# RWKV-7 stage of a hybrid decoder: 32x32 inverses by transposes on VectorE, smaller projection pieces, and two engines in written order

## The chip, the cores and the metric

The kernel runs on one core of a Trainium2 chip. The metric is the device time of one execution in microseconds. The engines are TensorE (PE; PEld is its weight load), VectorE (DVE), ScalarE (ACT), GpSimd (POOL) and SyncE (SP); ACTq, SPq and POOLq are the DMA issues in those engines' queues.

## The reference

Two decoder layers of width 1024 over 256 positions. Each layer is a SwiGLU block, a mixer and a second SwiGLU block, each followed by a LayerNorm. The mixer of layer 0 is a gated spatial MLP, that of layer 1 is RWKV-7 with 16 heads of 64. The change touches the latter alone:

```python
def step(state, inp):                       # per position t, per head
    r_t, w_t, k_t, v_t, a_t, b_t = inp
    sa = jnp.einsum('bhij,bhj->bhi', state, a_t)
    state = (state * w_t[:, :, None, :] + sa[..., None] * b_t[:, :, None, :]
             + v_t[..., None] * k_t[:, :, None, :])
    y = jnp.einsum('bhij,bhj->bhi', state, r_t)
    return state, y
...
r, k, v = jnp.einsum('nbsd,nde->nbse', x_rkv, w_rkv)
...
y = (y - mean) * lax.rsqrt(var + GN_EPS) * gn_g.reshape(H, N) + gn_b.reshape(H, N)
bonus = jnp.sum(r_h * k_h * r_k, axis=-1, keepdims=True) * v_h
out = ((y + bonus).reshape(bsz, seq, d).astype(x.dtype) * g) @ w_o
```

## The kernel before

The stages run in the order f00, sgu, f01, f10, rwkv, f11 (f = SwiGLU block). The 256 positions are two row blocks m of 128 partitions. Weights come through a stream of 512 KB pieces on the SP queue with four raw slots (L94); most are split into a rounded part wh (ScalarE, L118) and a rest wl (VectorE, L119), and a product takes three matmuls (L221 to L223). The R and V projections of RWKV use the raw fp32 piece directly (L301).

The recurrence is computed in four chunks of 64 positions (ch = 2m + c). Within a chunk the state update is a triangular system for each head; its matrix is inverted in 32x32 blocks. `ab` makes the matrix on TensorE (L988) and masks it on VectorE (L974) into Aab. GpSimd's DMAs write the diagonal blocks to DRAM (dA), and `inv_load` (ScalarE's queue) reads them back as M with one block of 32x32 per partition. Then 31 steps (i0 to i30, L1034 and L1036) run on VectorE for all 128 blocks at once. `inv_out` sends the inverse H, and its transposed copy (L1049), through DRAM (dH, dG) back to the head layout as Hf and G. `od` and `oe` (offdiag, L1079, and offdiag2, L1094) are the products that fill the off-diagonal block of each 64x64 inverse.

For each chunk there are then: `sc` (score matrices, L1013, masked into A), `x` (state times query, L1138), `av` (L1129), `u` (inverse times X, L1155, to VU), `s` (next state, L1165 and L1171), `rs` and `y` (outputs, L1148 and L1178). X<-X,mm (L1140) is the addition on VectorE that `u` of a chunk waits for. Behind them, for each row block, come `on` (group norm in two halves e of the heads: sum L1219, subtract L1221, square on ScalarE L1222, sum L1224, the power -0.5 on GpSimd L259, multiply L1227), `bo` (value times bonus, vb, L931), `og` (L1234 to L1236), `ga` (output gate, L1206), `oc` (transposes) and the output product `O` (eight k for each m). `rdone` ends an R projection: it multiplies R by the decay Ep and computes the bonus (L906 to L909). `dc` (decay_x) makes the shifted decay Ex by DMAs in ScalarE's queue (L821, L822).

What sets the order: a table ORDER of operation names is the order in which the stage's instructions are written. PE and the SP queue keep it. VectorE, ScalarE and GpSimd are ordered by a scheduler that may move an instruction ahead of others that it doesn't depend on. In the names, the digits are m, then c or the column half, then a piece: R011 is piece 1 of half 0 of block 1.

Of the kernel before, what the change touches and what calls it, by code (L numbers as in the profile page):

```python
# [56 lines left out]
class Stream:  # L57
# [80 lines left out]
class Builder:
# [529 lines left out]
    def rwkv(self, S):  # L668
# [230 lines left out]
        def rdone(h):  # L899
            def f(m, ps):  # L900
                if h == 0:
                    st["R"][m] = (st["E"][m][0], self.small(f"bonus{m}", [P, NH]))
                R, bo = st["R"][m]
                rk = self.s4("rk")[:, 0:512]
                s = slice(h * 512, h * 512 + 512)
                V.tensor_tensor(R[:, s], ps, st["E"][m][0][:, s], op=ALU.mult)  # L906
                V.tensor_tensor(rk, ps, st["kp"][m][:, s], op=ALU.mult)
# [115 lines left out]
        def inv_load():  # L1023
            st["M"] = self.s4("M")
            DI.dma_start(st["M"], self.dA.rearrange("b s t -> b (s t)"))

        def inv_step(s):
            def f():
                if s == 0:
# [4 lines left out]
                V.tensor_tensor(tv, H3[:, 0:s + 1, s:s + 1].broadcast_to([P, s + 1, n]),  # L1034
                                M3[:, s:s + 1, s + 1:32].broadcast_to([P, s + 1, n]), op=ALU.mult)
# [51 lines left out]
        def offdiag2(m):  # L1087
            def f():
                Q = st["Q"]
                ps = self.tpb()  # L1090
# [6 lines left out]
                for e in range(2):
                    d0 = e * 64
                    V.tensor_copy(st["Hf"][m].rearrange("p (b t) -> p b t", t=64)[d0:d0 + 32, :, 32:64],
                                  ps[d0:d0 + 32, :].rearrange("p (b t) -> p b t", t=32))  # L1100
# [5 lines left out]
        class Chunk:  # L1106
# [18 lines left out]

            def av(c_):
# [292 lines left out]
```

## Time and profile before

| | before |
|---|---|
| time, median of 3 runs | 1145.75 us (1145.54 to 1149.62) |
| the profiled execution | 1143.73 us, span 1142.0 us |
| TensorE | busy 1103.9 us (97% of the span), mean granted clock 0.988 |
| VectorE | busy 698.7 us (61%) |
| ScalarE | busy 480.5 us (42%) |
| GpSimd | busy 42.2 us (4%) |
| RWKV stage | 724.9 to 946.1 us from the span's start |

Busy time is the time in which at least one instruction of the engine runs. [...] A stretch of TensorE has lost time where it is not busy or where its clock is below 1.00.

### The profile page before, as it was taken

The numbers are of one execution on the slowest core, as the hardware profiler recorded it, in microseconds if no ns is written. First come the engines' busy times: TensorE is split into PE (matmuls) and PEld (weight loads), VectorE is DVE, ScalarE is ACT, GpSimd is POOL, SyncE is SP. The second block draws the span as 40 slices with busy tenths as digits, with TensorE's granted clock in tenths as the row PEclk, the third lists the DMA queues.
The fourth block names the chain that finished last, engine by engine and source line by source line (L and its number), as shares of the span: only waits on it lengthen the run. The fifth ranks groups of instructions, "written<-read, shape, count | busy, mean of one in ns | idle before, by whom it ended". The sixth has DMA issues, their size and how long they took to land.

```text
span 1142.0 us, 15347 instructions
## 1 busy us (share of the span) xinstructions
PE 1103.9 (97%) x5860; PEld 879.1 (77%) x5860; DVE 698.7 (61%) x969; ACT 480.5 (42%) x636; POOL 42.2 (4%) x44
## 2 busy tenths in 40 slices
PE   8999999999999999999999999999989889999997
PEld 5888888778888788888888888775555668788885
DVE  6654556769658555457655453878655787555544
ACT  5544443455335444444444452462123245444430
POOL 0000000100000000000000000112100110000000
PEclk9999999999999999999999999999999989999999
DMA  8776565775645766655677563437876146766530
GB/s 289 236 235 185 185 197 168 232 268 196 208 148 155 240 206 198 186 183 157 197 221 225 183 202 124 166 93 256 271 203 237 43 129 191 239 204 196 184 111 38
DMA packets 153933, 216.51 MB, mean 190 GB/s; under 512 B 21213, under 2 KB 114845, under 8 KB 153858
## 3 DMA queue, kind: packets, MB, share of 16 engines
q1 hardware_dynamic: 152394, 210.80, 57.7%
q0 software_dynamic: 1024, 3.15, 1.0%
q10 hardware_dynamic: 440, 1.57, 0.4%
q8 instruction: 46, 0.75, 0.3%
q14 instruction: 29, 0.24, 0.1%
HBM read 209.46 MB, written 3.42 MB: 186 GB/s over the span
## 4 chain that ended last, share of the span: by engine, by line
PE 81%; DVE 7%; DMA 5%; issue 2%; ACT 2%; POOL 1%; ACTq 0%; SPq 0%; DVEq 0%; POOLq 0%
PE mm L221 15%; PE mm L223 15%; PE mm L222 15%; PE acc L221 8%; PE acc L222 8%; PE acc L223 8%; PE mm L301 3%; DMA raw<-ffn_w_in 2%; DVE wl L119 2%; PE tp L415 2%; POOL rs L259 1%; PE tp L235 1%; ACT wh L118 1%; DMA raw<-rwkv_w_rkv 1%; PE tp L577 1%
## 5 line engine op out<-in xcount | busy, mean ns | idle before, releaser
L119 DVE TENSOR_TENSOR wl<-raw,wh 128x1024 fp32r<-128x1024 f32 (+1 forms) x332 | 396.2, 1209 | 267.1 <-ACT wh L118 259.8
L118 ACT CAST wh<-raw 128x1024 fp32r<-128x1024 f32 (+1 forms) x332 | 340.3, 1041 | 340.8 <-PE acc L223 146.0
L221 PE MATMUL mm<-wh,xh 128*128 128x512 f32 x832 | 327.3, 393 | 5.5 <-ACT wh L118 2.4
L222 PE MATMUL mm<-wl,xh 128*128 128x512 f32 x832 | 324.7, 390 | 0.6 <-DVE wl L119 0.6
L223 PE MATMUL mm<-wh,xl 128*128 128x512 f32 x832 | 325.1, 391 | 0.2 <-DVE xl L228 0.2
L221 PEld LDWEIGHTS mm<-wh,xh 128*128 128x128 f32 x832 | 156.5, 188 | 41.5 <-ACT wh L118 3.9
L223 PEld LDWEIGHTS mm<-wh,xl 128*128 128x128 f32 x832 | 156.6, 188 | 34.6 <-DVE xl L228 1.9
L222 PEld LDWEIGHTS mm<-wl,xh 128*128 128x128 f32 x832 | 156.7, 188 | 33.1 <-DVE wl L119 1.3
L221 PE MATMUL acc<-wh,hT 128*128 128x512 f32 x352 | 141.4, 402 | 0.0
L222 PE MATMUL acc<-wl,hT 128*128 128x512 f32 x352 | 137.4, 390 | 0.0
L223 PE MATMUL acc<-wh,hT 128*128 128x512 f32 x352 | 137.4, 390 | 0.0
L404 ACT ACTIVATE h<-mm 128x256 f32<-128x256 f32 x88 | 33.8, 384 | 106.0 <-PE mm L223 105.9
L223 PEld LDWEIGHTS acc<-wh,hT 128*128 128x128 f32 x352 | 66.1, 188 | 14.8
L222 PEld LDWEIGHTS acc<-wl,hT 128*128 128x128 f32 x352 | 66.2, 188 | 12.6
L221 PEld LDWEIGHTS acc<-wh,hT 128*128 128x128 f32 x352 | 66.1, 188 | 12.7
L405 DVE TENSOR_TENSOR h<-h,mm 128x256 f32<-128x256 f32 x88 | 36.8, 418 | 59.8 <-ACT h L404 59.8
L301 PE MATMUL mm<-raw,mix 128*128 128x512 f32 x128 | 59.4, 609 | 0.9 <-DMA raw<-rwkv_w_rkv 0.9
L259 POOL TENSOR_TENSOR rs<-ve,mhalf 128x1 f32<-128x1 f32 x14 | 14.2, 1011 | 926.2 <-DVE ve L267 926.2
L301 PEld LDWEIGHTS mm<-raw,mix 128*128 128x128 f32 x128 | 23.6, 193 | 26.6 <-issue 23.8
L228 DVE TENSOR_TENSOR hT<-tp,hT 128x512 fp32r<-128x512 f32 x44 | 30.2, 686 | 7.6 <-ACT hT L227 7.6
L227 ACT CAST hT<-tp 128x512 fp32r<-128x512 f32 x44 | 25.9, 588 | 9.0 <-PE tp L415 8.9
L227 ACT CAST xh<-tp 128x512 fp32r<-128x512 f32 x24 | 13.2, 588 | 34.9 <-PE tp L235 34.9
(193 smaller groups left out, 884.2 us busy)
## 6 DMA issues: line engine op xcount, KB each, us to landing
raw<-ffn_w_in SPq DMA_DIRECT2D x352, 256.0 KB, 4.0
raw<-ffn_w_out SPq DMA_DIRECT2D x88, 512.0 KB, 4.2
raw<-rwkv_w_rkv SPq DMA_DIRECT2D x40, 512.0 KB, 3.9
raw<-sgu_w_in SPq DMA_DIRECT2D x32, 512.0 KB, 5.6
raw<-sgu_w_out SPq DMA_DIRECT2D x16, 512.0 KB, 4.3
raw<-rwkv_w_o SPq DMA_DIRECT2D x8, 512.0 KB, 3.4
lng<-ln_g SPq DMA_DIRECT2D x6, 512.0 KB, 6.0
lnb<-ln_b SPq DMA_DIRECT2D x6, 512.0 KB
```

Of the source, the lines that this page charges most:

```text
L118: i = nc.scalar.copy(h[:, s], raw[:, s])
L119: j = nc.vector.tensor_tensor(l[:, s], raw[:, s], h[:, s].bitcast(F32), op=ALU.subtract)
L221: i = mm(out, lhsT=lh, rhs=rh, start=start, stop=False)
L222: mm(out, lhsT=lh, rhs=rl, start=False, stop=False)
L223: mm(out, lhsT=ll, rhs=rh, start=False, stop=stop)
L227: i = self.nc.scalar.copy(h, src)
L228: return i, self.nc.vector.tensor_tensor(l, src, h.bitcast(F32), op=ALU.subtract)
L259: self.nc.gpsimd.tensor_tensor(rs, v, self.mhalf[:, :w], op=ALU.pow)
L301: i = self.nc.tensor.matmul(ps, lhsT=xs[:, c], rhs=h[:, s], start=kk == 0, stop=kk == 7)
L404: nc.scalar.activation(hb[:, o + 256:o + 512], ps[:, 0:256], AF.Silu)
L405: nc.vector.tensor_tensor(hb[:, o:o + 256], hb[:, o + 256:o + 512], ps[:, 256:512], op=ALU.mult)
L415: nc.tensor.transpose(ps[:, o:o + P], st["h"][c][:, hh:hh + P], self.ident)
```

## The change

Five things are done in the RWKV stage.
1. The three round trips through DRAM (dA, dH, dG, 21 DMAs) are replaced by three transposes of 32x32 blocks on VectorE: M<-D before the steps, G<-H and Hd<-H behind them. `ab` masks into D (diagonal) and Aof (off-diagonal) in 128x256 pieces; ScalarE copies 32 rows of Aof into D. `inv_fill` (hf0, hf1) copies Hd into Hf, four copies on VectorE and four on GpSimd. The zeroing of Hf goes to GpSimd, and one half of oe's copy to ScalarE.
2. The R and V projections are emitted in quarter units (one weight piece) instead of half units, at new places among the chunks. In the chunks, `x` now stands ahead of `av`, so that X<-X,mm adds the result of av.
3. ScalarE copies an R projection out of PSUM (rk); the multiplication with Ep (`rm`) and the bonus (`rb`) are operations with places of their own.
4. The DMAs for Ex go into the SP queue instead of ScalarE's.
5. From iload on, each VectorE and ScalarE instruction of this stage is chained behind the one written before it (class Ordered). Weight splits, the splits of transposed blocks (xh, xl) and LayerNorms are not in this chain, and GpSimd's instructions are not.

```diff
+class Ordered:
+    def __getattr__(self, name):
+        fn = getattr(self.eng, name)
+
+        def f(*args, **kw):
+            i = fn(*args, **kw)
+            if self.on:
+                if self.last is not None:
+                    self.b.after(i, self.last)
+                self.last = i
+            return i
+        return f
...
+        V, A = Ordered(self, nc.vector), Ordered(self, nc.scalar)
...
-                masked(t[:, half(c)], ps, self.mask[:, 0:64])
...
-                        DA.dma_start(self.dA[b0:b0 + 16].rearrange("b s t -> s b t"),
-                                    t3[r0:r0 + 32, :, blk * 32:blk * 32 + 32])
+                p3 = ps.rearrange("p (b t) -> p b t", b=8)
+                for out, k in ((Of, 32), (D, 0)):
+                    V.tensor_tensor(out.rearrange("p (b t) -> p b t", b=8), p3[:, :, k:k + 32],
+                                    self.mask[:, k:k + 32].unsqueeze(1).broadcast_to([P, 8, 32]), op=ALU.mult)
+                for e in range(2):
+                    r = slice(e * 64 + 32, e * 64 + 64)
+                    A.copy(D[r, :], Of[r, :])
...
-            DI.dma_start(st["M"], self.dA.rearrange("b s t -> b (s t)"))
+            V.on = A.on = True
+            V.transpose(st["M"].rearrange("p (s t) -> p t s", s=32), st["D"].rearrange("p (b t) -> p t b", b=32))
...
+            (V.transpose(t.rearrange("p (b s) -> p s b", b=32), H.rearrange("p (s t) -> p s t", s=32)))
+            st["G"] = t
+            st["Hd"] = self.s4("Hd")
+            V.transpose(st["Hd"].rearrange("p (b t) -> p t b", b=32), H.rearrange("p (s t) -> p t s", s=32))
...
+                (V.tensor_copy if e else G.tensor_copy)(out, src)
...
-        DX, DW, DA, DI, DO = A, nc.sync, G, A, nc.sync
+        DX, DW = nc.sync, nc.sync
...
-                    for i in range(2):
+                    for i, us in enumerate(((0, 1), (2, 3)) if n == 1 else ((0,), (1,), (2,), (3,))):
...
-u1 rs1 ga01 s1 cR11 sc100 y0 vu11 sc101 y1 av2 sc110 x2 rs2 u2 sc111 un0 on00 on01 og00 y2 bo10 s2 av3 ga10 og01 x3
+mixG11 u1 R113 rb01 hf1 s1 g1_1 mixV10 y0 rm10 rm11 cR10 mixV11 y1 V010 cR11 V011 sc100 g2 p:gn_b V012 sc101 on00 V013 p:gn_g V110 on01 rb10 V111 bo00 rb11 V112 bo01 V113
+vu10 x2 av2 rs2 u2 vu11 s2 sc110 x3 sc111 ga00 av3 rs3 u3 gb ga01 un0 og00 y2 y3 og01 oc00 on10 O00 O10 on11 oc01 O20
```

Three places of the order matter. In the rows of the order, a row is one instruction: its number on its engine, its line, operation, outputs <- inputs and size; "x4" stands for four alike. Line 148 is the helper in class Ordered.

The first is VectorE where the inversion begins. Before, rows 550 to 557: the last mask of Aab, the mixes for later projections, what ends an R projection, and then the first step.

```order
550 L974 TENSOR_TENSOR Aab_6392<-tp,mask 128x512
551 L761 SCALAR_TENSOR_TENSOR mix_6490<-xx_5912,muT,xf_5911 128x128
552 L761 SCALAR_TENSOR_TENSOR mix_6378<-xx_5912,muT,xf_5911 128x128 x4
553 L906 TENSOR_TENSOR Ep_5936<-mm,Ep_5936 128x512
554 L907 TENSOR_TENSOR rk_6479<-mm,kp_5908 128x512
555 L908 TENSOR_TENSOR rk_6479<-rk_6479,r_k_6281 128x512
556 L909 TENSOR_REDUCE bonus_6327<-rk_6479 128x8
557 L1034 TENSOR_TENSOR T_6435<-H_6271,M_6433 128x31
```

After, the same place on VectorE:

```order
542 L148 TENSOR_TENSOR Aof_6271<-tp,mask 128x256
543 L148 TENSOR_TENSOR D_6270<-tp,mask 128x256
544 L148 TENSOR_TENSOR Aof_6271<-tp,mask 128x256
545 L148 TENSOR_TENSOR D_6270<-tp,mask 128x256
546 L148 STREAM_TRANSPOSE M_6411<-D_6270 128x32x32
547 L148 TENSOR_TENSOR T_6413<-H_6260,M_6411 128x31
```

The first step now stands right behind the last mask and the transpose; the mixes and the bonus have moved behind the inversion, and the multiplication of Ep into its middle.

The second place is VectorE ahead of the addition for chunk 2 (u2 waits for it). Before, rows 654 to 661: sums of the group norm of block 0, two masks of a score set, a subtraction, the addition, and the rest of the norm behind it.

```order
654 L1219 TENSOR_REDUCE sa<-acc 128x8 x2
655 L1220 TENSOR_SCALAR sa<-sa 128x8 x2
656 L974 TENSOR_TENSOR A_7218<-tp,mask 128x512
657 L974 TENSOR_TENSOR A_7219<-tp,mask 128x512
658 L1221 TENSOR_TENSOR yc_7301<-acc,sa 128x8x64
659 L1140 TENSOR_TENSOR X<-X,mm 128x512
660 L1221 TENSOR_TENSOR yc_7301<-acc,sa 128x8x64
661 L1224 TENSOR_REDUCE sb<-o_7302 128x8
```

After, 26 instructions stand between the masks of sc101 (rows 644 and 645) and the addition (row 672): the two halves of the norm, rows 646 to 657, the bonus rb10, rows 658 to 660, and these:

```order
661 L119 TENSOR_TENSOR wl_7149<-raw_7146,wh_7148 128x1024
662 L148 TENSOR_TENSOR vb_7174<-vb_6254,bonus_6320 128x512
663 L119 TENSOR_TENSOR wl_7171<-raw_7168,wh_7170 128x1024
664 L148 TENSOR_TENSOR vb_7174<-vb_7174,gn_b_7104 128x512
665 L148 TENSOR_TENSOR rk_6563<-rk_6563,kp_6053 128x512
666 L119 TENSOR_TENSOR wl_7185<-raw_7182,wh_7184 128x1024
667 L148 TENSOR_TENSOR rk_6563<-rk_6563,r_k_6852 128x512
668 L119 TENSOR_TENSOR wl_7202<-raw_7193,wh_7201 128x1024
669 L148 TENSOR_REDUCE bonus_6562<-rk_6563 128x8
670 L148 TENSOR_TENSOR vb_7174<-vb_6254,bonus_6320 128x512
671 L148 TENSOR_TENSOR vb_7174<-vb_7174,gn_b_7104 128x512
672 L148 TENSOR_TENSOR X<-X,mm 128x512
```

The norm is now whole ahead of the addition, and so are four weight splits of the output product and four vb products. Their weight pieces take the slots of the last V pieces.

The third place is TensorE between the last score set of chunk 2 and u2. Before, rows 3291 to 3296: scores, x, rs and u with nothing between.

```order
3291 L1013 MATMUL tp<-ZR_6315,KBT_6225 128x128 x8
3292 L1138 MATMUL mm<-S,ZR_6315 64x64 x8
3293 L1138 MATMUL mm<-S,ZR_6316 64x64 x8
3294 L1148 MATMUL acc<-S,ZR_6315 64x64 x8
3295 L1148 MATMUL acc<-S,ZR_6316 64x64 x8
3296 L1155 MATMUL tp<-X,Hf_6157 64x64 x16
```

After, the same place (L320 is a quarter unit, L1156 is x; av, rs and u of chunk 2 follow):

```order
3265 L1043 MATMUL tp<-ZR_6307,KBT_6219 128x128 x8
3266 L320 MATMUL mm<-raw_6976,mix_7022 128x512 x2
3267 L320 MATMUL mm<-raw_7074,mix_7022 128x512 x2
3268 L320 MATMUL mm<-raw_7084,mix_7022 128x512 x2
3269 L320 MATMUL mm<-raw_7108,mix_7022 128x512 x2
3270 L320 MATMUL mm<-raw_7139,mix_7022 128x512 x2
3271 L1156 MATMUL mm<-S,ZR_6306 64x64 x8
3272 L1156 MATMUL mm<-S,ZR_6307 64x64 x8
```

Five quarter units of V now stand there.

## Rows read from the trace of the kernel before

**Rows 1.** Windows: stretch, length, busy us of PE PEld DVE ACT POOL, PEclk, DMA, GB/s.
```profile
724.90:849.60 124.70, 115.29 (x626) 71.96 (x625) 94.67 (x220) 43.47 (x81) 17.66 (x20) 0.99 0.66 213
849.60:893.90 44.30, 40.90 (x726) 30.35 (x726) 23.18 (x36) 13.25 (x18) 0.00 (x0) 0.88 0.59 191
893.90:909.10 15.20, 11.04 (x212) 8.73 (x212) 13.03 (x23) 2.42 (x5) 3.61 (x2) 1.00 0.11 38
909.10:946.10 37.00, 32.50 (x182) 25.27 (x183) 30.11 (x44) 15.67 (x19) 5.05 (x3) 0.91 0.39 121
```

**Rows 2.** The timeline at 742 to 751: start, duration, engine, line, operation [idle before].
```profile
743.44 1.33 ACTq L821 DMA_DIRECT2D Ex<-Ep  x1
...
746.51 0.62 ACT L227 CAST mh<-mix 128x512 fp32r<-128x512 f32 x1 [2.61 <-DMA Ex<-Ep]
...
747.62 1.12 PE L799 MATMUL acc<-a,ah 65*128 65x512 f32 x2 [1.49 <-ACT ah L790]
```

**Rows 3.** The windows again: three short stretches.
```profile
748.00:754.00 6.00, 6.00 (x17) 4.00 (x16) 4.52 (x13) 4.53 (x7) 1.43 (x1) 0.72 0.03 10
852.00:860.00 8.00, 6.81 (x186) 6.31 (x181) 2.73 (x4) 1.69 (x4) 0.00 (x0) 0.50 0.83 270
932.00:938.00 6.00, 6.00 (x21) 4.75 (x20) 5.54 (x9) 2.23 (x4) 0.00 (x0) 0.59 0.30 87
```

**Rows 4.** The timeline of VectorE and TensorE around the inversion.
```profile
799.60 0.68 DVE L974 TENSOR_TENSOR Aab<-tp,mask 128x512 f32<-128x512 f32 x1
...
809.40 0.69 DVE L906 TENSOR_TENSOR Ep<-mm,Ep 128x512 f32<-128x512 f32 x1 [7.80 <-PE mm L301]
...
812.05 0.18 DVE L1034 TENSOR_TENSOR T<-H,M 128x31 f32<-128x31 f32 x1
...
838.59 0.22 DVE L1036 TENSOR_TENSOR H<-H,T 128x31 f32<-128x31 f32 x1
...
849.57 0.22 PE L1079 MATMUL tp<-G,Aab 32*32 32x32 f32 x2 [1.23 <-DMA G<-dG]
```

**Rows 5.** The chain of waits: start, duration, engine and work.
```profile
810.14 0.66 PE tp L235 x4
...
840.59 6.46 DMA dG<-M
...
847.53 2.51 DMA G<-dG
...
910.25 1.06 PE tp L1206 x2
...
912.36 2.01 PE acc L1178 x32
```

**Rows 6.** The groups by line of the stage, TensorE: busy us, mean ns | idle before.
```profile
L301 PE MATMUL mm<-raw,mix 128*128 128x512 f32 x128 | 59.4, 609 | 0.9 <-DMA raw<-rwkv_w_rkv 0.9
...
L1013 PE MATMUL tp<-ZR,KBT 64*128 64x128 f32 x128 | 10.5, 286 | 3.2 <-DVE VU L1160 1.6 <-ACT KBT L968 0.9 <-ACT ZR L953 0.7
```

**Rows 7.** The groups by line of the stage, VectorE.
```profile
L119 DVE TENSOR_TENSOR wl<-raw,wh 128x1024 fp32r<-128x1024 f32 x20 | 24.0, 1218 | 1.4 <-ACT wh L118 1.4
...
L974 DVE TENSOR_TENSOR A<-tp,mask 128x512 f32<-128x512 f32 x16 | 10.3, 686 | 4.1 <-PE tp L1013 3.9
...
L1049 DVE COPY M<-H 64x1024 f32<-64x1024 f32 x1 | 1.1, 1055 | 0.0
```

**Rows 8.** The timeline at 889 to 912, around the update of chunk 2.
```profile
894.45 0.63 ACT L1222 ACTIVATE o<-yc 128x512 f32<-128x512 f32 x1 [0.51 <-DVE yc L1221]
...
898.45 1.94 POOL L259 TENSOR_TENSOR rs<-sb,mhalf 128x8 f32<-128x8 f32 x1 [0.95 <-DVE sb L1225]
...
900.43 0.69 DVE L1227 TENSOR_TENSOR yc<-yc,rs 128x512 f32<-128x512 f32 x1 [1.53 <-POOL rs L259]
...
901.90 1.15 PE L1165 MATMUL tp<-VU,KB 128*64 128x64 f32 x32 [1.68 <-DVE A L974]
```

**Rows 9.** The timeline of TensorE at 925 to 934.
```profile
931.40 1.94 PE L235 MATMUL tp<-ident,o 128*128 128x128 f32 x8 [3.82 <-DVE o L1236]
```

More of the change, by code (lines that the diff above doesn't have):

```diff
@@ L902, in f, with rmul, rbonus @@
                     st["R"][m] = (st["E"][m][0], self.small(f"bonus{m}", [P, NH]))
[L903 to L907, printed above, removed]
+                    st["rk", m] = self.s4("rk")
+                s = half(h)
+                A.copy(st["rk", m][:, s], ps)
+            return f
+        def rmul(m, h):
+            def f():
+                R, s = st["R"][m][0], half(h)
+                (V.tensor_tensor(R[:, s], st["rk", m][:, s], R[:, s], op=ALU.mult))
+            return f
+        def rbonus(m, h):
+            def f():
+                s = half(h)
+                rk, bo = st["rk", m][:, s], st["R"][m][1]
+                (V.tensor_tensor(rk, rk, st["kp"][m][:, s], op=ALU.mult))
                 V.tensor_tensor(rk, rk, st["r_k"][:, s], op=ALU.mult)
@@ L1124, in vu, with x @@
                 return st["VU"][c_.ch][rows, h * 64:h * 64 + 64]
+            def x(c_):
+                c_.X = self.small("X", [P, 512])
+                if c_.ch:
+                    ps, S0 = self.mmb(), st["S", c_.ch]
+                    for h in range(NH):
+                        mm(ps[par(h), col(h)], lhsT=c_.zr(h, 0), rhs=S0[par(h), col(h)], start=True, stop=True,
+                           tile_position=((h % 2) * 64, (h % 2) * 64))
+                    A.copy(c_.X, ps)
             def av(c_):
@@ L1130, in av @@
                        tile_position=(c_.c * 64, (h % 2) * 64))
-                X = c_.X = self.small("X", [P, 512])
-                A.copy(X, ps)
-            def x(c_):
                 if c_.ch:
-                    ps, S0 = self.mmb(), st["S", c_.ch]
-                    for h in range(NH):
-                        mm(ps[par(h), col(h)], lhsT=c_.zr(h, 0), rhs=S0[par(h), col(h)], start=True, stop=True,
-                           tile_position=((h % 2) * 64, (h % 2) * 64))
                     V.tensor_tensor(c_.X, c_.X, ps, op=ALU.add)
+                else:
+                    A.copy(c_.X, ps)
             def rs(c_):
@@ L1389 @@
 ORDER = """
-p:k_k cm00 cm01 l1_0 lw00 mixK00 flush mixK01 K000 K001 cm10 cm11 la00 lw01 dec00 p:k_a dec01 dc0 mixK10 p:gn_g
-l1_1 mixV00 la01 la10 lw10 mixK11 K010 kp00 K011 lw11 zb00 kp10 K100 K101 kp01 dec10 zb01 cZ00 K110 hz cB00 dw0
-dec11 dc1 K111 zb10 la11 kp11 mixV01 V000 kn10 cB10 mixR00 mixG00 cB01 mixR01 V001 g1 zb11 ih kn11 kn00 cZ01 p:r_k
-ab00 R000 mixG01 cZ10 R001 cZ11 cB11 ab01 cR00 mixR10 V100 ab10 ab11 iload i0 g1_0 mixG10 R100 i1 i2 i3 R101 dw1
-mixV10 p:gn_b kn01 i4 cR01 i5 st0 mixG11 mixV11 V010 cK00 sc000 V011 i6 i7 i8 rs0 i9 kb1 g2 cK10 cK11 i10 i11 V101
-g1_1 cK01 i12 i13 i14 sc001 V110 i15 sc010 i16 kb0 V111 i17 mixR11 i18 i19 i20 i21 i22 i23 i24 i25 st1 vu00 sc011
-i26 i27 ga00 i28 i29 av0 vu01 x0 i30 iout R010 od0 od1 oe0 bo00 oe1 bo01 u0 gb R011 s0 R110 cR10 av1 vu10 x1 R111
-u1 rs1 ga01 s1 cR11 sc100 y0 vu11 sc101 y1 av2 sc110 x2 rs2 u2 sc111 un0 on00 on01 og00 y2 bo10 s2 av3 ga10 og01 x3
-rs3 u3 ga11 bo11 y3 oc00 O00 O10 on10 on11 oc01 O20 un1 og10 O30 og11 xw O40 O50 O60 O70 oc10 ln0 oc11 O01 O11 O21
+p:k_k cm00 cm01 l1_0 lw00 mixK00 flush mixK01 K000 K001 cm10 cm11 la00 lw01 dec00 p:k_a dec01 mixK10
+l1_1 mixV00 la01 la10 lw10 mixK11 dc0 K010 kp00 K011 lw11 zb00 kp10 K100 st0 K101 st1 kp01 dec10 zb01 cZ00 K110 cB00 dw0
+dec11 dc1 K111 zb10 la11 kp11 mixV01 V000 V001 kn10 cB10 mixR00 mixG00 cB01 mixR01 V002 V003 zb11 ih kn11 kn00 cZ01
+ab00 R000 R001 mixG01 cZ10 R002 R003 cZ11 cB11 ab01 mixR10 rm00 mixR11 ab10 ab11 iload i0 i1 cR00 R100 R101 i2 i3 cK00 i4 i5 i6
+cK10 V100 V101 i7 i8 kn01 i9 cK01 V102 V103 i10 i11 R102 R103 dw1 i12 i13 i14 hz R010 R011 i15 i16 rm01 cR01 i17 i18 i19 i20 sc000 R012 R013 i21 i22 i23
+cK11 i24 i25 rs0 kb0 vu00 kb1 R110 R111 i26 i27 i28 i29 i30 iout sc001 g1 od0 hf0 od1 oe0 x0 av0 oe1 u0 g1_0 vu01 sc010 p:r_k s0 sc011 x1 mixG10 rb00 R112 av1 rs1
+mixG11 u1 R113 rb01 hf1 s1 g1_1 mixV10 y0 rm10 rm11 cR10 mixV11 y1 V010 cR11 V011 sc100 g2 p:gn_b V012 sc101 on00 V013 p:gn_g V110 on01 rb10 V111 bo00 rb11 V112 bo01 V113
+vu10 x2 av2 rs2 u2 vu11 s2 sc110 x3 sc111 ga00 av3 rs3 u3 gb ga01 un0 og00 y2 y3 og01 oc00 on10 O00 O10 on11 oc01 O20
+bo10 ga10 O30 un1 bo11 ga11 og10 xw O40 og11 O50 O60 O70 oc10 ln0 oc11 O01 O11 O21
 O31 O41 O51 O61 O71
```

95 lines of the change are left out of this document (38 added, 57 removed).

## Prediction

> **What bounds the kernel now.** [...] The diff touches the RWKV stage alone, so I cut that stage, from its first transpose at 724.9 us to the next stage's first at 946.1, into four stretches by the table of windows [rows 1]. In each, idle is length less PE busy, and clock loss is length times (1 - PEclk), which is rough but adds up:
> - up to the off-diagonal product (od0) at 849.6: 9.4 idle, 1.2 clock;
> - to the update matmul of chunk 2 (u2) at 893.9: 3.4 and 5.3;
> - u2 to u3 at 909.1: 4.2 and 0;
> - u3 to the end of the stage: 4.5 and 3.3.
> Together 31.3 us. PE executes the same matmuls before and after, so the forecast is what becomes of these 31.3.
>
> Then the timeline at the waits. At 747.62 PE waits 1.49 for ah, because ScalarE's queue holds the Ex transfers: the first issue takes 1.33 us there, and the next cast starts 2.61 late, behind DMA Ex<-Ep [rows 2]. The clock then averages 0.72 for 6 us, 1.7 us lost [rows 3]. The inversion (31 steps on VectorE) starts at 812.05 although the last mask that it needs starts at 799.60; VectorE is idle for 7.80 of that, and what ends the idle time is a projection [rows 4]. The last step ends at 838.8, and od0 starts only at 849.57, after a wait of 1.23 on G<-dG [rows 4]; on the chain between them stand two transfers, 6.46 and 2.51 us [rows 5]. Projections hide most of this hole. Last, from 893.9 on there are no projections left to put between the chunks, and each short wait on VectorE shows.
>
> **The change, up to od0.** Gone are the round trips through DRAM and the 12.45 us between mask and first step. In their place: a transpose (M) before the steps and one (G) behind them. The trace of before has no such operation. Lower bound: L1049, a copy with swapped axes of 64x1024, 1.06 us [rows 7]; upper bound: twice that of a whole split (L119, 128x1024, 1.22 [rows 7]), 2.4. I take 1.1, since all three stream 1024 elements per partition. [...]
>
> VectorE from the end of ab11 on PE: two half-width masks and backlog about 2.5, the ScalarE copy into D about 0.5, M 1.1, the steps 22.9 (838.8 - 812.05 [rows 4] less the 6 score masks of that time at about 0.64), Em and Ep products 1.3, two score masks 1.3, G 1.1: 30.7. PE meanwhile has 14 quarter units. One unit is 4 matmul records; 32 units take 59.4 us in all [rows 6], 1.86 each, so 26.0. With six groups of four transposes (0.66 each [rows 5]) and two score sets (16 records each; 8 sets take 10.5 [rows 6], so 1.3 each) it comes to 32.6 at most, some 30 where they overlap. The two sides are level; I let PE lose 1 there. The Ex transfers move to the SP queue, behind and before weight loads; the stream runs up to four loads ahead, which hides some 5 us of issue (8 issues of 0.4 to 1.3); with that cover gone a load would be late by up to 3. The wait at 747 goes, with its clock loss. What other short waits remain, with 777 and the like, I put at 1.8. So **10.6 becomes 2.8: -7.8** (bounds -4.5, if the transposes cost 2.4 and SP delays a load by 1; -10.6, if nothing waits).
>
> Hidden by other engines' slack: 8 copies of D and 4 of rk on ScalarE, which is busy 43.47 of 124.7 us there [rows 1]; the Hf zeroing moved to GpSimd, which works 17.66 of 124.7. Without that slack they would add some 5 us to the mask path. The Hf copies by VectorE and GpSimd, the latter with no row of their kind (a VectorE 512-wide pass 0.69 [rows 7] below, GpSimd's 1.94 for a power [rows 8] above), have od0, od1, oe0 and av0 as cover, some 8 us.
>
> **od0 to u2.** Here the ten quarter units that are kept back (R112, R113 and V010 to V113) fill what PE waited for. I take idle 3.4 to 1, and leave the clock loss: the 32x32 matmuls of od and oe are still there, and the window 852 to 860 stood at 0.50 [rows 3]. **-2.4** (bounds 0 and -7, if the clock holds too).
>
> **u2.** This is where the written order bites. Between the masks of score set sc101 and the addition X<-X,mm that u2 waits for, VectorE before has only bits of the group norm on00/on01, chosen by the scheduler between urgent things. After, it must first go through all of on00, on01, rb10, the rest of rb11, four weight splits and four vb products. Each norm half is a chain through three engines: sum 0.65, scale 0.15, subtract 0.65, ScalarE's square 0.63 [rows 8], sum 0.65, scale 0.15, GpSimd's power 1.94 [rows 8], multiply 0.69, with hand-overs 5.8; in before VectorE waited 1.53 at its end [rows 8], and that was with other work between. Sum: masks 1.3, two halves 11.6, rb10 1.9, four splits 4.9 (1.22 each [rows 7]), four vb 2.5, three bonus operations 1.9, the addition 0.65: 24.7 us. PE has from the end of sc101: five quarter units 9.3, then x2, av2 and rs2, 32 small matmuls each as the set at 901.90 with its 1.15 [rows 8]: 12.7. So **PE stands for about 12 at u2**, where before lost 4.2 in the whole stretch [rows 1]. Behind u2 nothing of that is left on VectorE, and u2 to u3 should run without a wait. +7.8. A long wait before small matmuls cost clock at 931, after 3.82 idle [rows 9]: 0.59 over 6 us [rows 3], 2.5 lost; after 1.62 to 1.68 us (901.90 [rows 8]) nothing. I take half, +1.3. **u2: +9.1** (bounds +5 and +14).
>
> **The tail.** From u3 VectorE owes: VU 0.65, og0 3.8, four splits 4.9, two xl 1.3, on10 and on11 one behind the other 11.6, four vb 2.5, og1 3.8, one more split 1.2: 29.8. PE before took 18.5 from u3 to its wait (931.40 - 3.82 - 909.10) [rows 9]; after it has y2 (2.01) and two gates (2 x 1.06 each) [rows 5] more there: 24.7. oc10 waits about 5.1 against 3.82, since before on10 and on11 were interleaved, and oc00 or oc01, now closer behind their norms, some 0.7. Clock loss as before. **+2.0** (0 to +4).
>
> **Sum.** -7.8 - 2.4 + 9.1 + 2.0 = +0.9. The profiled execution took 1143.73 us (span 1142.0), 0.2% under the median of 1145.75; I add to the median: 1146.65, **1147**.
>
> **Rivals.**
> *The early gain wins (faster).* If the clock also holds through od and oe (5.3 back), because chunk 0 and 1 now have quarter units among them, and the norm halves go faster (power 1.66 rather than 1.94, hand-overs hidden): -5 to -8 more, 1139 to 1142, with all waits before od0 gone 1137. For it: the clock was at 1.00 from 893.9 to 909.1 despite 4.2 idle [rows 1]. It decides when the wait at u2 is under about 6 us: then the net is -5.7, or 0.5%, which is what a measurement here can tell from no change.
> *u2 decides (slower).* One mechanism: the stand of 12 us drops the clock, and u2, s2, x3, av3, rs3, u3 and the y products (some 17 us) then run at half of it; I let 7 of the 17 be lost, not all the 8.5: +7 rather than +1.3, so 1152.5; if VectorE comes late to sc101's masks by 3, 1156. Against it: the same clock row of 893.9 to 909.1. It decides when the wait is over about 16.
> *Transposes or shared ports (slower or same).* At 2.4 us each, two lie on the path to od0: +2.6, 1149.3. VectorE copying with GpSimd at once may also make them take turns: 4 copies of 0.69 and 4 of up to 1.94 one by one instead of side by side, +2.7 before u0, partly covered: 1149. [...]
> *The written order does nothing.* If the scheduler's order was the same, the u2 term falls away. The order of the rows shows that it is not.
>
> **How the numbers follow.** Even, within 0.5% (1140 to 1151.5): 0.42, with the transposes' rival inside. Faster: 0.33, as the early gain is direct and the clock at od unknown. Slower: 0.25. Range 1137 to 1156: from the faster rival with all waits gone to the slower with late masks. The likeliest case's own range is 1142 to 1151.
>
> **What would show it.** Right: first step near 795, od0 near 823, M, G, Hd at about 1.1 each; PE's longest wait at u2, 10 to 13 us, ended by X<-X,mm; oc10 waiting 6; no wait at 747 and at G. Wrong: od0 later than 828 (steps, or D, late); a wait at u2 under 6; a clock of 0.50 over more than 8 us behind it; waits on weight loads, which SP's added issues would cause.

## The result, and the profile after

The changed kernel takes 1154.87 us (median of 6 runs, 1151.88 to 1157.76), the kernel before 1145.12 (median of 6, 1143.35 to 1149.62). The ratio is 1.0081, 95% interval 1.0055 to 1.0108: slower by 0.8%. The forecast was 1147 with a range of 1137 to 1156. The range holds, the likeliest case does not: the time lies in the slower case, which had a chance of 0.25, between the 1152.5 and 1156 of its rival "u2 decides". All times and ratios here are of runs in the usual state; one execution of e4 (1392.61 us, mean clock 0.75) was in a slow one and is left out.

The profiled execution has a span of 1150.9 us, 8.9 more than before. First the line of busy times on its page, which shows that TensorE's busy time grew too, by 5.5 us for the same number of instructions:

```profile
PE 1109.4 (96%) x5860; PEld 884.2 (77%) x5860; DVE 704.6 (61%) x975; ACT 486.8 (42%) x650; POOL 39.8 (3%) x42
```

Then the windows of the changed kernel over the four stretches of the stage (columns as in [rows 1]). The stage starts at 723.30, od0 at 826.09, u2 at 894.56, u3 at 910.56, and the next stage at 954.70:

```profile
723.30:826.09 102.79, 96.22 (x506) 60.08 (x504) 81.93 (x192) 43.75 (x81) 14.21 (x14) 0.98 0.59 190
826.09:894.56 68.47, 56.57 (x820) 41.97 (x821) 42.43 (x74) 17.73 (x30) 5.89 (x6) 0.85 0.50 162
894.56:910.56 16.00, 14.24 (x196) 11.39 (x196) 5.34 (x8) 2.79 (x4) 0.00 (x0) 0.69 0.31 115
910.56:954.70 44.14, 37.98 (x222) 27.45 (x221) 36.77 (x54) 16.58 (x21) 4.21 (x3) 0.92 0.36 109
```

Against [rows 1] the stage is 10.2 us longer (231.4 for 221.2). Idle, length less busy, went from 9.4, 3.4, 4.2 and 4.5 to 6.6, 11.9, 1.8 and 6.2: in all 21.5 to 26.4, +4.9. The rest, +5.3, is busy time: the same matmuls took longer, and in three of the four stretches the granted clock (a share of full speed) is lower than before (0.98 for 0.99, 0.85 for 0.88, 0.69 for 1.00). So about half of the loss is waiting, and half is longer matmuls. od0 comes 21.9 us earlier from the stage's start (102.8 for 124.7), and u2 nevertheless 2.3 later (171.3 for 169.0): the time gained went to work moved behind od0, and to u2.

The timeline of the changed kernel around the inversion, VectorE and TensorE (start, duration, engine, line, operation, idle before). These answer to [rows 4]:

```profile
792.20 2.06 DVE L148 STREAM_TRANSPOSE M<-D 128x1024 f32<-128x1024 f32 x1 [1.67 <-ACT D L148]
794.29 0.19 DVE L148 TENSOR_TENSOR T<-H,M 128x31 f32<-128x31 f32 x1
...
800.88 0.63 PE L254 MATMUL tp<-ident,Em 128*128 128x128 f32 x4 [2.50 <-DVE Em L148]
801.34 8.73 PE L320 MATMUL mm<-raw,mix 128*128 128x512 f32 x16
...
810.73 0.69 DVE L148 TENSOR_TENSOR Ep<-rk,Ep 128x512 f32<-128x512 f32 x1 [2.95 <-ACT rk L148]
...
816.16 1.29 DVE L148 TENSOR_TENSOR A<-tp,mask 128x512 f32<-128x512 f32 x2 [1.30 <-PE tp L1043]
...
824.11 1.92 DVE L148 STREAM_TRANSPOSE G<-H 128x1024 f32<-128x1024 f32 x1
825.89 2.02 DVE L148 STREAM_TRANSPOSE Hd<-H 128x1024 f32<-128x1024 f32 x1
...
826.09 2.21 PE L1103 MATMUL acc<-G,Aof 32*32 32x32 f32 x128 [1.17 <-DVE G L148]
```

None of the round trips is left on this path, and the first step starts 71.0 us after the stage's start instead of 87.2. But a transpose takes 1.9 to 2.1 us, M waits 1.67 for ScalarE's copies into D, TensorE waits 2.50 for Em, and od0 still waits 1.17 for G. In the midst of the steps VectorE stands still twice, 2.95 us for rk (ScalarE's copy of a projection that TensorE had finished late) and 1.30 for a score set.

The timeline ahead of u2, which answers to [rows 8]. VectorE goes from the last masks of sc101 (870.39) through the norm, bonus and splits to X<-X,mm (893.74); TensorE waits twice:

```profile
870.39 1.29 DVE L148 TENSOR_TENSOR A<-tp,mask 128x512 f32<-128x512 f32 x2 [1.72 <-PE tp L1043]
...
876.65 0.69 DVE L148 TENSOR_TENSOR yc<-yc,rs 128x512 f32<-128x512 f32 x1 [1.85 <-POOL rs L278]
...
882.21 0.69 DVE L148 TENSOR_TENSOR yc<-yc,rs 128x512 f32<-128x512 f32 x1 [1.75 <-POOL rs L278]
...
893.74 0.68 DVE L148 TENSOR_TENSOR X<-X,mm 128x512 f32<-128x512 f32 x1
...
883.86 1.86 PE L1163 MATMUL mm<-VU,A 64*64 64x64 f32 x29 [3.31 <-ACT VU L148]
...
885.57 1.96 PE L1176 MATMUL acc<-S,ZR 64*64 64x64 f32 x31
894.56 1.97 PE L1183 MATMUL tp<-X,Hf 64*64 64x64 f32 x32 [7.03 <-DVE X L148]
```

From 870.39 to 894.42 are 24.0 us; 24.7 was worked out. The 3.31 is av2, whose VU copy stands on ScalarE behind two casts of output weights. The 7.03 is u2 itself. A set of 32 small matmuls takes 1.97 here against 1.15 at [rows 8], and the windows of two us say why (the column behind the busy times is the granted clock):

```profile
882.00:884.00 2.00, 0.14 (x2) 0.14 (x4) 1.75 (x3) 2.00 (x3) 0.18 (x1) 0.97 0.50 201
884.00:886.00 2.00, 2.00 (x41) 2.00 (x43) 1.97 (x3) 2.00 (x3) 0.00 (x0) 0.50 0.03 8
...
902.00:904.00 2.00, 2.00 (x30) 1.78 (x30) 1.29 (x2) 0.00 (x0) 0.00 (x0) 0.50 0.00 0
904.00:906.00 2.00, 1.67 (x30) 1.41 (x26) 0.30 (x1) 0.59 (x1) 0.00 (x0) 0.91 0.00 0
```

The granted clock falls to 0.50 at the end of the first wait (0.97 from 882 to 884) and stays there until 904, for 20 us.

### The profile page after: what moved, and what is told of

It reads as the page before. It is cut to its first block, busy times and chain, and to the rows that moved or that the text cites. A ratio compares the mean times of both kernels' runs of the same rounds, so it can differ in the third digit from the quotient of the medians.

```text
span 1150.9 us, 15343 instructions
## 1 busy us (share of the span) xinstructions
PE 1109.4 (96%) x5860; PEld 884.2 (77%) x5860; DVE 704.6 (61%) x975; ACT 486.8 (42%) x650; POOL 39.8 (3%) x42
## 3 DMA queue, kind: packets, MB, share of 16 engines
HBM read 208.15 MB, written 2.11 MB: 183 GB/s over the span
## 4 chain that ended last, share of the span: by engine, by line
PE 83%; DVE 8%; DMA 3%; issue 2%; ACT 2%; POOL 1%; SPq 0%; DVEq 0%; ACTq 0%; POOLq 0%
PE mm L240 15%; PE mm L242 15%; PE mm L241 15%; PE acc L240 8%; PE acc L242 8%; PE acc L241 8%; PE mm L320 2%; DVE wl L119 2%; DMA raw<-ffn_w_in 2%; PE tp L434 2%; PE tp L254 1%; ACT wh L118 1%; DVE yc L148 1%; PE tp L1043 1%; PE tp L805 1%
## 5 line engine op out<-in xcount | busy, mean ns | idle before, releaser
L240 PEld LDWEIGHTS acc<-wh,hT 128*128 128x128 f32 x352 | 66.2, 188 | 12.7
L320 PE MATMUL mm<-raw,mix 128*128 128x512 f32 x128 | 60.4, 614 | 0.3 <-DMA raw<-rwkv_w_rkv 0.3
L320 PEld LDWEIGHTS mm<-raw,mix 128*128 128x128 f32 x128 | 23.5, 194 | 26.8 <-issue 24.0
```

What stands on the lines that cost most here:

```text
L240: i = mm(out, lhsT=lh, rhs=rh, start=start, stop=False)
L320: i = self.nc.tensor.matmul(ps, lhsT=xs[:, c], rhs=h[:, s], start=kk == 0, stop=kk == 7)
```

## The experiments

Theory A: the loss stands at u2, made by the written order ahead of X<-X,mm and by the low clock behind it. Theory B: it lies elsewhere (transposes, od and oe, the extra work at the end), and u2 only passes it on. All ratios are to the kernel before. Positions are counted from the stage's start, which itself varies by 4 us between executions (722.0 to 726.0); they are read, to within 0.2 us and from one execution of each kernel, from the first matmul of od0, u2, u3 and the next stage:

| kernel | od0 | u2 | u3 | next stage | ratio (95% interval) |
|---|---|---|---|---|---|
| before | 124.7 | 169.0 | 184.2 | 221.2 | 1 |
| changed | 102.8 | 171.3 | 187.3 | 231.4 | 1.0081 (1.0055 to 1.0108) |
| e1, scheduler's order | 103.0 | 165.3 | 182.5 | 220.7 | 0.9980 (0.9969 to 0.9992) |
| e2, u2 cleared | 102.7 | 160.4 | 177.4 | 221.5 | 1.0019 (1.0000 to 1.0039) |
| e3, 10 unread matmuls | 102.6 | 171.9 | 187.8 | 232.0 | 1.0083 (1.0064 to 1.0102) |
| e4, before with Ex on SP | 127.1 | 173.3 | 188.5 | 224.5 | 1.0012 (0.9994 to 1.0031) |
| e5, 13 unread matmuls | 103.0 | 171.5 | 184.2 | 228.3 | 1.0048 (1.0032 to 1.0064) |
| e6, u2 cleared, free from u3 | 102.8 | 159.2 | 177.7 | 216.6 | 0.9950 (0.9933 to 0.9967) |
| e7, M twice | 105.6 | 174.1 | 190.3 | 234.7 | 1.0120 (1.0088 to 1.0152) |
| e8, e6 with Em and D earlier | 104.2 | 162.0 | 179.5 | 217.7 | 0.9960 (0.9941 to 0.9978) |
| e9, e2's table, scheduler's order | 103.2 | 165.6 | 182.3 | 220.5 | 0.9999 (0.9984 to 1.0014) |
| e10, only the norm earlier | 102.9 | 161.5 | 179.1 | 224.1 | 1.0005 (0.9991 to 1.0019) |

**e1, the changed kernel without the written order.**

```diff
-            V.on = A.on = True
```

> The changed kernel without its last part: VectorE and ScalarE are again ordered by the scheduler, all else is as changed. Theory A (the loss is the written order ahead of u2: VectorE needs 24.0 us from the masks of sc101 to X<-X,mm and TensorE has 12 us of work there): the scheduler puts some nine instructions fewer ahead of that addition, about 15 us of work, so the two waits at u2 (3.3 and 7.0 us) fall to about 1 and the clock stays at 1.00 behind them; 1140 to 1145. Theory B (the loss is elsewhere: the transposes at 2 us each, TensorE's low clock around od and oe, the gates at the end): 1152 to 1156, as changed. If the written order is worth something in the inversion itself, od0 comes later than 826 and eats the gain.

Measured: 1142.59 us. VectorE and TensorE ahead of u2 in e1's timeline, and one of its windows behind u2:

```profile
871.43 1.29 DVE L148 TENSOR_TENSOR A<-tp,mask 128x512 f32<-128x512 f32 x2 [1.72 <-PE tp L1043]
...
886.46 0.68 DVE L148 TENSOR_TENSOR X<-X,mm 128x512 f32<-128x512 f32 x1
...
887.28 1.15 PE L1182 MATMUL tp<-X,Hf 64*64 64x64 f32 x32 [3.07 <-DVE X L148]
```

```profile
890.00:892.00 2.00, 0.68 (x12) 0.68 (x14) 1.24 (x2) 0.00 (x0) 0.00 (x0) 0.50 0.84 311
```

The same stretch on VectorE is 15.7 us for 24.0, and u2 runs at full clock (1.15). od0 is where it was, so the written order is worth nothing in the inversion; it costs 6.0 us up to u2 and, from u3 to the end, 44.1 for 38.2. Theory A stands for its first half: this one line is the whole difference in sign. What it said of the clock does not hold: a wait of 3.07 us is left at u2, and the clock falls behind it, to 0.50 from 890 to 898 (the set of 32 small matmuls at 896.08 takes 1.97 us); u2 to u3 takes 17.2 us for 16.0.

**e2, the written order kept, and what u2 doesn't need moved away from it.**

```diff
-... y1 V010 cR11 V011 sc100 g2 p:gn_b V012 sc101 on00 V013 p:gn_g V110 on01 rb10 V111 bo00 rb11 V112 bo01 V113
-vu10 x2 av2 rs2 u2 vu11 s2 sc110 x3 sc111 ga00 av3 ...
+... y1 on00 V010 cR11 V011 sc100 g2 p:gn_b V012 on01 sc101 V013 p:gn_g V110 V111 V112 V113
+vu10 x2 av2 rs2 u2 vu11 rb10 s2 bo00 sc110 x3 rb11 sc111 ga00 bo01 av3 ...
```

> The changed kernel with the table edited: on00 right behind y1, on01 ahead of sc101, and rb10, bo00, rb11, bo01 behind u2; written order kept. Between the last mask of sc101 and X<-X,mm there is then one weight split instead of 26 instructions. Theory A: no wait over 2 us at u2, clock 1.00 there, 1139 to 1144, under the kernel before. Theory B: the instructions only move, and the same time is lost at sc111, x3 or oc10; 1150 to 1156.

Measured: 1146.32 us, above what theory A gave. The place is cleared, as e2's timeline shows:

```profile
885.54 1.15 PE L1183 MATMUL tp<-X,Hf 64*64 64x64 f32 x32 [0.82 <-DVE X L148]
```

u2 comes 10.9 us earlier, and only 9.9 of these are left at the end: u2 to u3 takes 17.0 us for 16.0, since two waits for VU stand behind u2 (0.83 and 1.73) and the clock, which theory A had at 1.00, falls in the second:

```profile
890.00:892.00 2.00, 2.00 (x30) 1.85 (x26) 1.90 (x4) 0.00 (x0) 0.00 (x0) 0.50 0.92 338
```

That the whole is no faster than before has another reason, and it stands in the windows of e2 from u3 on: 44.12 us as in the changed kernel, where e1 has 38.2 and the kernel before 37.0.

```profile
902.49:946.61 44.12, 38.02 (x222) 27.44 (x221) 36.76 (x54) 16.59 (x21) 4.21 (x3) 0.92 0.35 108
```

So the written order loses at two places, at u2 and in the tail, some 6 us at each by e1.

**e10, only the norm moved.** The first part of e2's edit (on00 and on01), without the bonus operations.

```diff
-... y1 V010 cR11 V011 sc100 g2 p:gn_b V012 sc101 on00 V013 p:gn_g V110 on01 rb10 V111 ...
+... y1 on00 V010 cR11 V011 sc100 g2 p:gn_b V012 on01 sc101 V013 p:gn_g V110 rb10 V111 ...
```

> The changed kernel with on00 right behind y1 and on01 ahead of sc101, and the bonus operations left where they are: about half of e2's edit. Between the last mask of sc101 and X<-X,mm stand then 9.3 us of splits, vb and bonus and 1.9 of rb10, 12 us against TensorE's 12.5: if the count of the work on VectorE is right, the wait at u2 is 2 us or less but for the 0.7 of e2, and the time is within 2 us of e2 (1146.3): 1145 to 1149. If the waits inside the norm on ScalarE and GpSimd weigh less than I think, more of the 10.3 us stays: 1150 to 1154.

Measured: 1146.05 us, no different from e2. Its u2 waits 1.21. The norm's place is the one that counts: behind y1 VectorE was idle in the changed kernel, waiting 6.97 and 1.72 us for score sets.

**e3 and e5, unread matmuls in the waits at u2.** Nothing that the output needs is left out.

```diff
-vu10 x2 av2 rs2 u2 vu11 ...
+vu10 x2 fill4 av2 rs2 fill6 u2 vu11 ...
...
+            ps = self.tpb()
+            for i in range(n):
+                mm(ps, lhsT=self.ident, rhs=st["R"][1][0][:, 0:512], start=True, stop=True)
```

> The changed kernel with ten more matmuls whose results nobody reads (128 columns of weights against 512 columns), four behind x2 and six ahead of u2, 0.93 us each at full clock: they lie in the 10.3 us in which TensorE waits at u2, so that the wait stays and only the clock behind it can change. If the clock (0.50 from 884 to 904) costs what the 20 us suggest, 4 to 6 us come back: 1148 to 1151, and the row of 896 to 904 shows 1.00. If the wait itself is all of the loss, 1154 to 1157.

Measured: 1153.96 us, as changed. The filling was too short, and the timeline and windows of e3 show that the clock still fell:

```profile
895.91 1.97 PE L1183 MATMUL tp<-X,Hf 64*64 64x64 f32 x32 [3.14 <-DVE X L148]
```

```profile
892.00:894.00 2.00, 0.78 (x2) 0.00 (x0) 2.00 (x4) 0.00 (x0) 0.00 (x0) 1.00 0.76 217
894.00:896.00 2.00, 0.09 (x2) 0.12 (x4) 1.73 (x3) 0.00 (x0) 0.00 (x0) 0.83 0.84 260
896.00:898.00 2.00, 1.88 (x32) 1.69 (x32) 0.00 (x0) 0.08 (x1) 0.00 (x0) 0.50 1.03 397
```

It settles nothing by itself, so e5 has `fill9` for `fill6`.

> As e3_warm_u2 with nine unread matmuls instead of six ahead of u2, so that no wait is left there (in e3 3.1 us were left and the clock fell in them, at 895, and stayed at 0.50 until 905). X<-X,mm still ends where VectorE has it, near 171 us after the stage's start. If the low clock behind the wait costs time, u2 to u3 falls from 15.9 us to 13 to 14 and the whole to 1150 to 1152; if the small matmuls there are bound by something else, it stays at 1154.

Measured: 1152.62 us; 0.9967 of the changed kernel by the two ratios, but their intervals overlap, so that the gain in the whole is not clear of noise. The windows of e5 from u2 to u3:

```profile
894.66:907.35 12.69, 10.64 (x196) 8.14 (x197) 5.34 (x8) 2.79 (x4) 0.00 (x0) 1.00 0.37 140
```

u2 starts where it did (171.5), since VectorE sets it, and the stretch behind it takes 12.69 us instead of 16.00 with the clock at 1.00. So of the loss at u2 the low clock behind the wait is 3.3 us, read from one execution of each. Of the versions that hold the change e5 alone has no low clock there, and its 12.7 us are the shortest; before, the stretch took 15.2 with waits of its own.

**e7, the transpose M done twice.**

```diff
-            V.transpose(st["M"]...
+            for i in range(2):
+                V.transpose(st["M"]...
```

> The changed kernel with the transpose M<-D done twice, to the same place. If VectorE's chain sets od0 (its wait for G is 1.17), od0 comes later by the 2.07 us of the transpose, 104.9 after the stage's start, and the whole by 2: 1156 to 1158. If the projections set it, nothing moves: 1154 to 1155.

Measured: 1159.70 us. The pair takes 4.28 us in its timeline:

```profile
791.22 4.28 DVE L148 STREAM_TRANSPOSE M<-D 128x1024 f32<-128x1024 f32 x2 [1.67 <-ACT D L148]
```

od0 is 2.8 later and the next stage 3.3; the first step is 2.2 later, and the wait for rk is 4.06 for 2.95. So time added to VectorE's chain is lost in full at od0. That a transpose of 1.1 us would have gained as much is not shown.

**e4, the kernel before with one part alone: Ex issued by SP.**

```diff
-        DX, DW, DA, DI, DO = A, nc.sync, G, A, nc.sync
+        DX, DW, DA, DI, DO = nc.sync, nc.sync, G, A, nc.sync
```

> The kernel before with one part alone: the Ex transfers are issued by SP instead of ScalarE. My sum has 1.5 us of wait and 1.7 us of clock at 747 for it: 1141 to 1143 where before takes 1145. Rival: the wait at 747 goes, but the work ahead of od0 ends on the round trip through DRAM anyway, so that the time gained is given back before 849: 1144 to 1146. Second rival: SP's eight issues make a weight load late, 1146 to 1149.

Measured: 1145.92 us (median of nine), no difference. The wait of [rows 2] is gone, but ten us later there is a new one in e4's timeline:

```profile
758.96 0.50 PE L222 MATMUL mm<-wl,mh 128*128 128x512 f32 x1 [2.93 <-DVE wl L119]
```

The split was late on VectorE, which had worked on kk, kp and a ahead of it (the preparation of the keys). The gain is given back before od0, more fully than the first rival said: od0 is at 127.1.

**e6, a version for both places: e2, and the scheduler's order again behind u3.**

```diff
-... av3 rs3 u3 gb ga01 ...
+... av3 rs3 u3 free gb ga01 ...
...
+... "free": lambda: (setattr(V, "on", False), setattr(A, "on", False)),
```

> e2_u2_clear, and the written order ends behind u3: from there VectorE and ScalarE are the scheduler's again. In e2 u3 came 6.8 us earlier than before (counted from the stage's start), and 7.1 us were lost again from u3 to the end, where the norm halves on10 and on11 stand one behind the other; e1_free_order took 38.2 us there and e2 44.1. Theory A, for the tail as for u2: the tail takes 38 to 39, 1138 to 1141, below both kernels. Rival: the tail is bound by TensorE's extra work there (y2 and two gates), and takes 42 to 44; 1144 to 1147.

Measured: 1140.69 us, ratio 0.9950 (0.9933 to 0.9967): faster than both kernels. Windows of e6 from u2 on, and its longest wait in the tail:

```profile
881.58:900.10 18.52, 14.98 (x193) 12.14 (x193) 17.03 (x24) 4.11 (x6) 0.00 (x0) 0.66 0.62 200
900.10:939.02 38.92, 36.60 (x230) 26.64 (x228) 32.20 (x49) 16.84 (x21) 4.51 (x3) 0.99 0.39 119
```

```profile
926.77 0.63 PE L254 MATMUL tp<-ident,o 128*128 128x128 f32 x4 [1.10 <-DVE o L148]
```

The tail is 38.9 against 44.1: TensorE is idle for 2.3 us in it instead of 6.2, and its busy time is 36.6 instead of 38.0 at a clock of 0.99 instead of 0.92. In e6's timeline VectorE goes through on10 and on11 interleaved again. u2 to u3, in e2's order, takes 18.5 us here, at a clock of 0.66, so that part of the loss is still there. The rival (TensorE's own work binds the tail) is out.

**e8, e6 with Em and D earlier.**

```diff
-cK10 V100 V101 i7 i8 kn01 i9 ...
+cK10 V100 V101 i7 i8 i9 ...
...
-... iload i0 i1 cR00 R100 R101 i2 i3 cK00 ...
+... iload i0 i1 cR00 R100 R101 i2 i3 kn01 cK00 ...
...
-                    A.copy(D[r, :], Of[r, :])
+                    (V.tensor_copy if m and c else A.copy)(D[r, :], Of[r, :])
```

> e6_clear_tail, kn01 seven steps earlier (TensorE waited 2.5 us for it at 800.9), and the last copy into D on VectorE instead of ScalarE (M waited 1.67 for it). VectorE's chain to G is about 1 us shorter, and the wait for Em goes; since od0 hangs on G, most of the 2.5 turns into a longer wait there. 1 us less than e6 if theory A holds for the chain, the same if the earlier kn01 only delays the first steps.

Measured: 1141.37 us, no better than e6. The wait for Em is gone, and two waits for weight pieces have come in its timeline:

```profile
805.18 3.34 PE L320 MATMUL mm<-raw,mix 128*128 128x512 f32 x4 [2.26 <-DMA raw<-rwkv_w_rkv]
...
810.63 5.42 PE L320 MATMUL mm<-raw,mix 128*128 128x512 f32 x12 [2.10 <-DMA raw<-rwkv_w_rkv]
...
813.27 0.69 DVE L148 TENSOR_TENSOR Ep<-rk,Ep 128x512 f32<-128x512 f32 x1 [5.70 <-ACT rk L148]
```

od0 was to come 1 us earlier and came 1.4 later. e8's chain of waits (start, duration, work) has one load of weights of 11.50 us, and behind it the projection; so VectorE waits 5.70 for rk in the midst of the steps, where it waited 2.95.

```profile
799.08 11.50 DMA raw<-rwkv_w_rkv
```

Why this load took so long stays open.

**e9, e2's table in the scheduler's order.**

```diff
-            V.on = A.on = True
...
+... y1 on00 V010 cR11 V011 sc100 g2 p:gn_b V012 on01 sc101 V013 p:gn_g V110 V111 V112 V113
+vu10 x2 av2 rs2 u2 vu11 rb10 s2 bo00 sc110 x3 rb11 sc111 ga00 bo01 av3 rs3 u3 gb ga01 ...
```

> The edited table of e2 with no written order at all. It tells whether the chain through the instructions is worth anything once the table no longer puts the norm ahead of u2. If the written order helps up to u3 (e2 reached u3 at 177.4 us from the stage's start, e1, the changed table in the scheduler's order, at 182.5), this is slower than e6 by 2 to 5 us: 1142 to 1146. If the table alone does it: 1139 to 1142.

Measured: 1144.70 us, so slower than e6 (0.9999 for 0.9950, intervals apart). u3 is at 182.3 for e6's 177.7. Two waits in e9's timeline stand on VectorE, whose order was the scheduler's:

```profile
825.83 2.42 PE L1102 MATMUL acc<-G,Aof 32*32 32x32 f32 x128 [3.19 <-DVE G L148]
...
871.38 2.67 PE L1043 MATMUL tp<-ZR,KBT 64*128 64x128 f32 x16 [2.75 <-DVE A L148]
```

The first is no loss against e6, since od0 comes at 103.2 for 102.8. The second is new: masks of a score set that the scheduler put off, behind which the 16 matmuls of the next set take 2.67 us for 1.16 in e6. So a written order is worth some 4 us up to u3, if the table is right.

## Why the prediction was right and wrong

**What bounds, and the method.** Counting idle and clock by stretch found the places. The rule "length times (1 - PEclk)" overstates: by it the clock loss of the stage went from 9.9 us to 20.8, +10.9, where the sum of busy time grew by only 5.3. A set of 32 small matmuls at half the clock takes 1.97 us for 1.15, not twice; and the rule also counts the wait of 7.03 us ahead of u2, where the clock stood at 0.50 and no matmul ran (busy 0.00 from 888 to 894).

**Up to od0: the overlap failed, and the transposes were mis-sized.** I put 2.8 us of lost time; idle alone was 6.6, and od0 came 102.8 us after the start where I had 98. The step that failed is "the two sides are level; I let PE lose 1 there": VectorE's 30.7 us and TensorE's 30 were taken to run side by side, and they wait for each other. From the end of ab11 on TensorE (789.71) to od0 are 36.4 us for the 30.7. The largest part of the difference is the 4.3 us in which VectorE stands still between steps, 2.95 for rk and 1.30 for a score set, where I had nothing. Ahead of them TensorE waits 2.50 for Em: kn01 stands nine steps into the inversion, and cK01 on TensorE needs it. Behind that wait the clock falls in this execution (0.50 from 802 to 804), and 16 projection matmuls take 8.73 us where e1, without the wait, has 7.13; the projection that VectorE then waits for comes behind them. In e3 the same wait is 2.57 us long and the same 16 matmuls behind it take 7.03, so the wait alone does not make the clock fall; od0 is at 102.6 there too, with a weight load 1.77 late in between. That TensorE's wait made VectorE's is read from this order, not tested alone: in e8, where the wait for Em is gone, weights come late in its place. M and G are 4.0 for 2.2, the wait for ScalarE's copies into D is 1.67 where I had 0.5 of copying (the copy of a ZR block stood between them), and the masks are 0.8 for 2.5; the steps and products came out as worked out.

The transposes took 2.06, 1.92 and 2.02 us where I took 1.1, an estimate from the 1.06 of L1049 [rows 7]: the same 1024 elements per partition did not take the same time. Two on the path to od0 are 1.8 more. All three lie nearer the upper bound that I gave, 2.4. Both their inputs and their outputs step by 32 elements, and no run has a transpose without such steps, so whether the steps make the difference stays open. The wait at 747 is gone, as I said; that by itself it saves 3.2 is refuted by e4 for the kernel before.

**od0 to u2, without u2's own wait: right.** Idle beside the two waits was 1.6 against 1; the clock around od and oe stayed low (0.65 from od0 to 836.68), as taken.

**u2: the mechanism right, the clock mis-sized.** VectorE's 24.7 us were 24.0, TensorE's wait of 12 was 10.3, in two pieces: the first of them, ScalarE's VU copy behind weight casts, I had not seen. e1 and e2 take most of it away, to 3.7 and 1.5 us, by taking away the instructions, so the cause is shown. I took half of a known clock loss, 1.3; by e5 it was 3.3, and in e3, with 3.14 us of wait left there, the clock fell too. Nor did u2 to u3 run without a wait: 1.8 idle, so that the +7.8 of idle came out by two errors that cancel. The rival "u2 decides" had the clock's mechanism right, and one sign of being wrong came, 0.50 over more than 8 us behind the wait. Its condition, a wait over about 16, did not hold, and its 7 us were 3.3; that the time lies within its 1152.5 to 1156 is in part luck, since the loss up to od0 is not in it.

**The tail: right.** 5.1 us were forecast at oc10 and 0.7 at oc00 or oc01; measured 2.63 and 2.11 at oc10's two groups of transposes (4.7) and 1.4 behind oc00. I gave it to the extra gates and the serial norm halves; e6 shows that 5 of the 44 us are the written order in this stretch, and that the halves one behind the other are the reason within it is read from the timeline, not tested alone.

```profile
938.39 1.05 PE L254 MATMUL tp<-ident,o 128*128 128x128 f32 x4 [2.63 <-DVE o L148]
941.54 1.09 PE L254 MATMUL tp<-ident,o 128*128 128x128 f32 x4 [2.11 <-DVE o L148]
```

**The copies side by side: a small price.** Beside GpSimd's copies of Hd, VectorE's pair of them takes 1.27 us; the same pair for the other half, at 854.80 with GpSimd idle, takes 0.86:

```profile
829.07 1.27 DVE L148 COPY Hf<-Hd 32x512 f32<-32x512 f32 x2
...
828.06 2.75 POOL L1091 COPY Hf<-Hd 32x512 f32<-32x512 f32 x4 [2.92 <-DVE Hd L148]
...
854.80 0.86 DVE L148 COPY Hf<-Hd 32x512 f32<-32x512 f32 x2
```

So the rival of copies that take turns has a sign, but of 0.4 us where I gave it 2.7, a supposition with no row of before; and TensorE has no wait for these copies. What GpSimd's copies take without VectorE's beside them no run shows. Why the pair takes longer beside them the records do not tell.

**The sum.** Idle was to change by +0.8 us in all and changed by +4.9; nearly all of the difference stands up to od0, where 6.6 us were idle and I had 2.8 at most. Busy time was to stay and grew by 5.3, of which e5 gives 3.3 to the clock behind u2. Another 1.6 stands within the wait at u2 and lengthens nothing: av2 and rs2 take 3.7 us there (883.86 to 887.53), av3 and rs3 at full clock 2.1 (908.56 to 910.64). And 1.6 stands behind the wait for Em, against which the low clock at 748 [rows 3] is gone.

## What to carry to other kernels

Before an engine's order is fixed by hand, count, for each instruction that the bounding engine waits for, what stands ahead of it in the new queue, and compare that with the bounding engine's own work over the same stretch: here 24 us against 12. Put a chain that crosses three engines where its own engine would be idle anyway (behind y1), not ahead of an urgent operation, and let the scheduler have the stretches where two such chains should interleave. Where two engines feed each other within a stretch, follow the chain from one to the other and back instead of taking the longer of the two sums: here TensorE's 2.5 us for Em stood ahead of VectorE's 4.3. A wait costs its length and can also cost the clock of the small matmuls behind it, 3.3 us here, which the trace's idle column does not show; but with the wait gone the next ones behind it can still cost the clock, as in e1, e2 and e6 (0.70, 0.80 and 0.66 from u2 to u3, which takes 17.2, 17.0 and 18.5 us for e5's 12.7 at 1.00). And a transfer taken off a path gives nothing if a later operation on the same path, here a split on VectorE, was as late.

## What the runs showed of the hardware that was not expected

- A transpose of 32x32 blocks over 128x1024 fp32 on VectorE takes 1.92 to 2.06 us in the changed kernel and 2.14 in e8, about twice the 1.06 of a copy of 64x1024 with swapped axes [rows 7].
- In e3 the granted clock fell to 0.50 within a wait of 3.14 us (0.83 from 894 to 896, 0.50 from 896), and u2 behind it took 1.97 us. In e1 a wait of 3.07 us at the same place left u2 at 1.15 us, and the clock fell only behind u2 (0.50 from 890 to 892). Behind the wait for Em it fell after 2.50 us in the changed kernel (0.50 from 802 to 804), and in e3 not after 2.57 (a mean of 1.00 up to od0). In these runs the length of one wait alone does not decide it.
- VectorE copies 32x512 fp32 in 0.42 us while GpSimd is idle, and in 0.52 and 0.74 beside GpSimd's copies of the same size. GpSimd takes 0.60 to 0.69 for one there, where its power of 128x8 takes 1.64 to 1.98.
